# A group softmax bound by DMA: the first store waits until the fourth load has landed on every engine

## The chip, the cores and the metric

One NeuronCore of a Trainium2 chip. The metric is the device time of one execution in microseconds (us), the median of several. A profile gives one execution in detail; its span is some 2 us shorter than the time of the same execution.

## The reference

```python
B, N, D, G = 4, 4096, 4352, 8            # x is float32, 285 MB
x_g = x.reshape(B, N, G, D // G)         # groups of 544
exp = np.exp(x_g - x_g.max(axis=-1, keepdims=True))
out = (exp / exp.sum(axis=-1, keepdims=True)).reshape(B, N, D)
```

16,384 rows of 4,352 numbers are read once and written once, 570 MB in all.

## The kernel before

A tile is 128 partitions of two rows each, 4,352 KB. There are 64 tiles in five buffers. SyncE issues all transfers into one queue: four loads first, then for each tile t the store of t and the load of t + 4. I call them load 0 to load 63 and store 0 to store 63. In the queue the order is load 0, 1, 2, 3, store 0, load 4, store 1, load 5, and so on; from store 0 to store 60 every transfer changes direction against the one before it. I call such a change a turn.

```python
def take(engine, sem, n=1):
    engine.sem_inc(sem, -n).wait_op(sem, n, "sem-ge")
...
def load(t, source):
    nc.sync.dma_start(out=bufs[t % NT][:, :], in_=source).then_inc(landed[t % NT], 16)

def store(t, target):
    take(nc.sync, scaled, R)
    nc.sync.dma_start(out=target, in_=bufs[t % NT][:, :]).then_inc(stored[t % NT], 16)

def step(t, source, target):
    store(t, target)
    take(nc.sync, stored[(t - 1) % NT], 16)
    load(t + AHEAD, source)

for t in range(AHEAD):                    # AHEAD = 4, NT = 5
    load(t, xt[t])
nc.sync.sem_inc(stored[NT - 1], 16)
with nc.sync.Fori(0, ring_turns) as u:    # 12 ring turns of five steps
    for t in range(NT):
        step(t, turn_in[u, t], turn_out[u, t])
...
```

VectorE takes the maximum of each group and later multiplies by the reciprocal of the sum; ScalarE takes the exponential and the sum. Row by row this costs VectorE 9.6 us.

Of the kernel before, what the change touches and what calls it, by code (L numbers as in the profile page):

```python
# [1 line left out]

# [4 lines left out]


@with_exitstack
def kernel(  # L10
    ctx: ExitStack,
    tc: tile.TileContext,
    x: bass.AP,
    out: bass.AP,
):
    nc = tc.nc
    G = 8
    P = 128
    R = 2
    NT = 5  # L20
    S = R * NT
    AHEAD = NT - 1
    xf = x.flatten_outer_dims()
    of = out.flatten_outer_dims()
    N, D = xf.shape
    Dg = D // G
    nt = N // (P * R)
    nr = nt * R
    turns = (nr - 1) // S
    ring_turns = (nt - AHEAD) // NT  # L30
    steps = ring_turns * NT
    f32 = mybir.dt.float32
    X = mybir.AxisListType.X
    Exp = mybir.ActivationFunctionType.Exp
    xt = xf.rearrange("(t p r) d -> t p (r d)", p=P, r=R)
    ot = of.rearrange("(t p r) d -> t p (r d)", p=P, r=R)
    turn_in = xf[AHEAD * P * R:(AHEAD + steps) * P * R, :].rearrange(
        "(u b p r) d -> u b p (r d)", b=NT, p=P, r=R)
    turn_out = of[:steps * P * R, :].rearrange("(u b p r) d -> u b p (r d)", b=NT, p=P, r=R)

    landed = [tc.alloc_semaphore(f"landed{b}") for b in range(NT)]
    stored = [tc.alloc_semaphore(f"stored{b}") for b in range(NT)]

    max_done = tc.alloc_semaphore("max_done")
    exp_done = tc.alloc_semaphore("exp_done")
    rec_done = tc.alloc_semaphore("rec_done")
    scaled = tc.alloc_semaphore("scaled")

    ctx.enter_context(tc.tile_critical(no_gpsimd_drain=True))  # L49
    bufs = [ctx.enter_context(nc.sbuf_tensor(f"xt{b}", [P, R * D], f32)) for b in range(NT)]  # L50
    mx = ctx.enter_context(nc.sbuf_tensor("mx", [P, S, G], f32))
    sm = ctx.enter_context(nc.sbuf_tensor("sm", [P, S, G], f32))
    rs = ctx.enter_context(nc.sbuf_tensor("rs", [P, S, G], f32))

    def take(engine, sem, n=1):
        engine.sem_inc(sem, -n).wait_op(sem, n, "sem-ge")

    def row(s):
        b, r = divmod(s, R)
        return bufs[b][:, r * D:(r + 1) * D].rearrange("p (g d) -> p g d", g=G)  # L60

    def vector_max(s):
        i = nc.vector.reduce_max(out=mx[:, s, :], in_=row(s), axis=X, negate=True)  # L63
        if s % R == 0:
            i.wait_op(landed[s // R], 16, "sem-ge")
        i.then_inc(max_done, 1)

    def vector_scale(s):
        nc.vector.reciprocal(out=rs[:, s, :], in_=sm[:, s, :]).wait_op(  # L69
            exp_done, s + 1, "sem-ge").then_inc(rec_done, 1)  # L70
        xr = row(s)
        nc.vector.tensor_tensor(  # L72
            out=xr,
            in0=xr,
            in1=rs[:, s, :].unsqueeze(2).to_broadcast([P, G, Dg]),
            op=mybir.AluOpType.mult,
        ).wait_op(rec_done, s + 1, "sem-ge").then_inc(scaled, 1)

    def scalar_exp(s):
        xr = row(s)  # L80
        for g in range(G):
            i = nc.scalar.activation(  # L82
                out=xr[:, g, :],
                in_=xr[:, g, :],
                func=Exp,
                bias=mx[:, s, g:g + 1],
                scale=1.0,
                accum_out=sm[:, s, g:g + 1],
            )
            if g == 0:  # L90
                i.wait_op(max_done, s + 1, "sem-ge")
        i.then_inc(exp_done, 1)
# [14 lines that stand above are left out]
    for t in range(AHEAD):  # L107
        load(t, xt[t])
    nc.sync.sem_inc(stored[NT - 1], 16)
    with nc.sync.Fori(0, ring_turns) as u:  # L110
        for t in range(NT):
            step(t, turn_in[u, t], turn_out[u, t])
    for t in range(steps, nt):
        if t + AHEAD < nt:
            step(t, xt[t + AHEAD], ot[t])
        else:
            store(t, ot[t])
    for t in range(nt - NT, nt):
        nc.sync.wait_ge(stored[t % NT], 16)

    nc.scalar.preload_act_table(Exp)  # L121
    with nc.scalar.Fori(0, turns):
        for s in range(S):
            scalar_exp(s)
        nc.scalar.sem_inc(max_done, -S)
    for n in range(turns * S, nr):
        scalar_exp(n % S)


    vector_max(0)  # L130
    with nc.vector.Fori(0, turns):
        for s in range(S):
            if s == S - 1:
                for b in range(NT):
                    nc.vector.sem_inc(landed[b], -16)
            vector_max((s + 1) % S)
            vector_scale(s)
        nc.vector.sem_inc(exp_done, -S)
        nc.vector.sem_inc(rec_done, -S)
    for n in range(turns * S, nr):  # L140
        if n + 1 < nr:
            vector_max((n + 1) % S)
        vector_scale(n % S)


# [1 line left out]
_INS = ['x']  # L147
_OUTS = [((4, 4096, 4352), 'float32')]


# [23 lines left out]
```

## Time and profile before

| | before |
|---|---|
| time, median | 1330.15 us (1329.7 to 1330.15, 3 runs) |
| DMA queue, share of 16 engines | 99.7% |
| VectorE / ScalarE busy | 91% / 58% |
| one transfer, on the engine that is ahead | 10.28 us |

The prediction below shows the lines of the profile. Every transfer is spread over 16 DMA engines, and each of them adds one to the transfer's semaphore when its part has landed. The trace has the time of each increment. I call the first of the sixteen the leading engine's landing, the last one the straggler's, and the difference the spread. The trace also has each packet of 34,816 bytes with its duration, 1,024 for each engine, median 1.288 us. What a packet takes beyond that I call its excess; summed over a stretch of time and divided by 16 it is the time lost by an average engine. Packets don't carry an engine's number, so I can't say which engine is the straggler. A busy engine can be followed all the same, since each of its packets starts within a few ns of the end of the one before.

### The profile page before, as it was taken

How to read it: one execution, taken by the hardware profiler on the slowest of the kernel's cores; microseconds unless marked ns; L12 is line 12 of the kernel's file. 1: busy time of each engine (PE TensorE's matmuls, PEld its weight loads, DVE VectorE, ACT ScalarE, POOL GpSimd, SP SyncE). 2: the span in 40 equal slices, each digit the busy share in tenths (PEclk: the TensorE clock that was granted, in tenths of full speed). 3: DMA queues.
4: the chain of work that ended last, by engine and by line, in shares of the span. 5: the costliest groups of instructions: out<-in, count | busy, mean ns of one | idle time of the engine just before them, and what ended most of it. 6: DMA issues, size and time to landing. Idle time of an engine off the chain costs nothing. (4 is left out here: it accounts for less than half of the span.)

```text
span 1326.8 us, 3155 instructions
## 1 busy us (share of the span) xinstructions
DVE 1207.7 (91%) x384; ACT 764.4 (58%) x2049; POOL 0.2 (0%) x4
## 2 busy tenths in 40 slices
DVE  5999999999898898998988989889899898998984
ACT  3666565655565555655655556555565555655652
POOL 0000000000000000000000000000000000000000
DMA  9999999999999999999999999999999999999998
GB/s 403 419 431 433 429 430 430 436 433 429 431 433 436 433 431 430 435 435 436 431 431 433 436 433 433 430 432 436 435 433 429 433 436 436 431 430 433 435 435 358
DMA packets 18435, 570.46 MB, mean 430 GB/s; under 512 B 2048, under 2 KB 2048, under 8 KB 2048
## 3 DMA queue, kind: packets, MB, share of 16 engines
q1 hardware_dynamic: 18432, 570.43, 99.7%
q14 instruction: 3, 0.02, 0.0%
HBM read 285.21 MB, written 285.21 MB: 430 GB/s over the span
## 5 line engine op out<-in xcount | busy, mean ns | idle before, releaser
L82 ACT ACTIVATE xt<-xt,mx 128x544 f32<-128x544 f32 x1024 | 751.3, 734 | 539.2 <-DVE mx L63 539.2
L63 DVE TENSOR_REDUCE mx<-xt 128x8 f32<-128x4352 f32 x128 | 599.1, 4681 | 94.8 <-DMA xt<-in_x_dram 94.8
L72 DVE TENSOR_TENSOR xt<-xt,rs 128x4352 f32<-128x4352 f32 x128 | 600.6, 4692 | 4.4
L82 ACT ACTIVATION_READ_ACCUMULATOR xt<-xt,mx 128x1 f32 x1024 | 191.0, 187 | 0.0
L69 DVE RECIPROCAL rs<-sm 128x8 f32<-128x8 f32 x128 | 24.6, 193 | 2.6 <-ACT xt L82 2.6
L121 ACT ACT_TABLE_LOAD x1 | 1.3, 1283 | 0.9 <-SPq L49 0.9
L158 POOL MEMSET const-bfloat16-1.0<- 128x1 bf16 x1 | 0.1, 101 | 0.0
L158 POOL MEMSET const-uint8-127<- 128x1 uint8 x1 | 0.1, 101 | 0.0
L158 POOL MEMSET const-float32-0.0<- 128x1 f32 x1 | 0.1, 98 | 0.2 <-issue 0.2
L158 POOL MEMSET const-float32-1.0<- 128x1 f32 x1 | 0.1, 98 | 0.0
## 6 DMA issues: line engine op xcount, KB each, us to landing
xt<-in_x_dram SPq DMA_DIRECT2D x64, 4352.0 KB, 30.6
out_dram<-xt SPq DMA_DIRECT2D x64, 4352.0 KB, 40.3
```

The costliest lines, as they stand in the source:

```text
L63: i = nc.vector.reduce_max(out=mx[:, s, :], in_=row(s), axis=X, negate=True)
L69: nc.vector.reciprocal(out=rs[:, s, :], in_=sm[:, s, :]).wait_op(exp_done, s + 1, "sem-ge").then_inc(rec_done, 1)
L72: nc.vector.tensor_tensor(out=xr, in0=xr, in1=rs[:, s, :].unsqueeze(2).to_broadcast([P, G, Dg]), op=mybir.AluOpType.mult,).wait_op(rec_don ...
L82: i = nc.scalar.activation(out=xr[:, g, :], in_=xr[:, g, :], func=Exp, bias=mx[:, s, g:g + 1], scale=1.0, accum_out=sm[:, s, g:g + 1],)
L121: nc.scalar.preload_act_table(Exp)
L158: nc = _bacc.Bacc("TRN2", target_bir_lowering=False, num_devices=1)
```

## The change

The intent: the first store starts on all DMA engines together, since it is issued only when the last of the four first loads has landed on all of them.

```diff
     for t in range(AHEAD):
         load(t, xt[t])
     nc.sync.sem_inc(stored[NT - 1], 16)
+
+    nc.sync.wait_ge(landed[AHEAD - 1], 16)
     with nc.sync.Fori(0, ring_turns) as u:
```

## The prediction

> **What bounds the kernel now.** I read the page first (busy shares, DMA slices, queues), then SyncE's part of the timeline, the chain that ended last, the windows of the last 30 us, and last the sixteen completion increments that the trace holds for each transfer. The page:
>
> ```profile
> span 1326.8 us, 3155 instructions
> DVE 1207.7 (91%) x384; ACT 764.4 (58%) x2049; POOL 0.2 (0%) x4
> ...
> GB/s 403 419 431 433 429 430 430 436 433 429 431 433 436 433 431 430 435 435 436 431 431 433 436 433 433 430 432 436 435 433 429 433 436 436 431 430 433 435 435 358
> ...
> q1 hardware_dynamic: 18432, 570.43, 99.7%
> ...
> xt<-in_x_dram SPq DMA_DIRECT2D x64, 4352.0 KB, 30.6
> out_dram<-xt SPq DMA_DIRECT2D x64, 4352.0 KB, 40.3
> ```
>
> The one queue that carries all loads and stores occupies the 16 DMA engines for 99.7% of the span. VectorE is second at 91%. There are 64 loads and 64 stores of equal size, and a store lands 40.3 us after its issue because it stands behind earlier work in the queue. The kernel is bound by DMA. VectorE could become the bound only if DMA got 9% faster.
>
> How little is left: the trace holds 16,384 packets of 34,816 bytes, 1,024 for each engine, median 1.288 us. Eight of them are an engine's part of one transfer, and on the engine that is ahead one transfer follows the other at 10.28 us. 34,816 B / 1.286 us = 27.07 GB/s for one engine, 433 GB/s for sixteen. Only the first two slices and the last one of the GB/s row are clearly below that. SyncE's timeline shows what happens in the first:
>
> ```profile
> 0.96 1.99 SPq L96 DMA_DIRECT2D xt<-in_x_dram  x4
> 39.24 0.37 SPq L100 DMA_DIRECT2D out_dram<-xt  x1
> 39.86 0.35 SPq L96 DMA_DIRECT2D xt<-in_x_dram  x1
> 58.06 0.35 SPq L100 DMA_DIRECT2D out_dram<-xt  x1
> 58.67 0.35 SPq L96 DMA_DIRECT2D xt<-in_x_dram  x1
> ```
>
> Four loads (load 0 to 3) are issued at once; store 0 follows at 39.24, when tile 0 is scaled, and load 4 right behind it. Load 3 lands only at 45.08 to 46.00 (first to last engine). So store 0 is queued some 6 us before it can start, and each engine goes on to it by itself.
>
> The sixteen increments give the spread between the first and the last engine: 0.55, 0.54, 0.53 us for loads 0 to 2, 0.93 for load 3, 0.68 for store 0, 1.29 for load 4, then rising to 3.3 (150 us), 4.2 (210 us), 5.0 (318 us), and it stays at 5.0 until the end. One straggler causes the last 1.5 us or so of it: of the sixteen, the last but one is at 3.3 to 3.7. The end shows what it costs:
>
> ```profile
> 1310.00:1315.00 5.00, 0.00 (x0) 0.00 (x0) 0.00 (x0) 1.00 1.02 439
> 1315.00:1320.00 5.00, 0.00 (x0) 0.00 (x0) 0.00 (x0) 1.00 1.02 439
> 1320.00:1325.00 5.00, 0.00 (x0) 0.00 (x0) 0.00 (x0) 1.00 0.26 111
> ```
>
> Columns are the stretch, its length, VectorE, ScalarE and GpSimd work, clock, DMA share and GB/s. The last store lands on the first engine at 1321.09 and on the last at 1325.48; DMA share falls to 0.26 while the straggler finishes. The chain of waits ends like this:
>
> ```profile
> 1253.72 30.64 DMA xt<-in_x_dram
> ...
> 1284.39 4.68 DVE mx L63
> ...
> 1298.54 5.97 ACT xt L82 x16
> ...
> 1304.78 4.69 DVE xt L72
> ```
>
> The last load lands on the last engine at 1284.37, 25.1 us of compute follow, and the last store is issued at about 1309.56. The leading engines end the store before it near 1309.8 (landed 1310.16), so they starve for about 0.6 us; the straggler (landed 1315.20) does not. The straggler alone sets the end.
>
> **What the Trainium skill says.** Page "DMA: Bandwidth & Descriptors", section "Why a DMA increments its semaphore by 16 and not by 1": up to 16 engines finish independently and each posts one increment after its data. The trace agrees: 16 increments for each of the 128 transfers, up to 5.04 us apart. The same page, "Anatomy of one DMA": DMA engines do not wait on semaphores; a wait is on the issuing sequencer before dispatch. So the new wait can only delay the issue, and shows up as empty queues. Same page, "Where 436 GB/s comes from": a ceiling of 435.2 GB/s; the trace's steady 433 agrees, so nothing is to be had from rate. Same page, "Latency and other measured facts": about 600 ns to the first byte of a transfer issued from SyncE; the trace has 1.02 us for the first load (issue 0.96, first packet 1.98) and 0.8 us for the last store (1309.56 to 1310.38), and I use those.
>
> **The change part by part.** One wait is added; in the built program it sits on the branch into the loop, so no instruction is added, and nothing moves on the other engines.
>
> 1. The wait. Store 0 is ready at 39.24 and now goes after load 3 has landed on all engines. In its place are: (a) Without company in the queue, load 3 should take 10.28 us after load 2 (33.97 to 34.50), so it lands at 44.3 to 44.8. (b) From there to the first packets of store 0: the last store is the same case, with VectorE's end at 1309.47 and first packets at 1310.38 to 1310.47, 0.9 us; I add 0.2 for the branch into the loop. First packets at 45.9. (c) Store 0 then needs 10.28 + 0.35 us (last packet to increment, from 1325.13 to 1325.48): lands at about 56.5, within some 0.2 us on all engines. Before: 55.61 to 56.29. The leading engine loses 0.9 us, the straggler 0.2 us.
>
> 2. What pays for it. The last two packets of load 3 are long in the trace, 1.3 to 2.2 us against 1.288 (starts 41.2 to 43.5, about 2 us after store 0 and load 4 were issued). This cost the leading engine 11.11 - 10.28 = 0.8 us and the straggler 46.00 - 34.50 - 10.28 = 1.2 us. I take it that these vanish. So the hole of about 2 us (43.9 to 45.9 on a leading engine) is more than half paid by them.
>
> 3. The alignment. After 56.3 the straggler loses 5.04 - 0.68 = 4.4 us more against the leader. Its last increments show where: +0.4 at load 4, +0.3, +0.6, +0.5, +0.7 at the next loads, then +0.8 near 214 and +0.6 near 318, never at a store. The packets agree: long ones come in groups at 64, 85, 105, 126, 147 us, each the last packets of a load before the engine turns to a store, and the later an engine arrives, the longer (at 64.0 us +0.06, at 64.9 us +0.49). Nothing of this needs the start of store 0 to be staggered: each turn from load to store makes its own delay, and groups stop when the engines have moved apart. If so, beginning at 0.2 instead of 0.68 us only means that the spread grows again to about the same size.
>
> Sum: the leader goes from 55.61 to 56.5, all turns after that are the same, and the final spread decides. At 5.0 us again the end comes 0.9 us later; at 4.2, 0.1 us later; at 3.3 us, 0.8 us earlier. Compute does not enter: store 1 is issued at 58.06 when its tile is scaled, as before, and tile 4 is needed by VectorE only near 86 us, against a landing at 67.
>
> **The rivals.** First, the intent holds: engines that begin together stay together, the spread stays under 1 us to the end. Then the end is 0.2 - 4.4 = about -4 us: 1326. For it: loads 0 to 2 do keep a spread of 0.54. Against it: these are load after load; the spread grows at every turn from load to store, and there are 64 of them. Second, being aligned makes the turn at load 4 as dear as the one at load 3 was (all sixteen in step, 0.8 to 1.2 us each), and the spread ends at 6 to 7: +1.5 to +2.5 us, 1332. For it: the dear turn was the one with the smallest spread. Third, the hole delays the supply: load 5 waits for store 0. Store 0 now lands at 56.5, and load 5 was issued at 58.67 behind store 1 anyway, so this is hidden: 0. Fourth, VectorE as bound: it gets its first tile at 13.90 as before and waits only later; 0.
>
> **Range and chances.** I weigh: same final spread (0 to +1 us) 0.4, smaller spread (-2 to 0) 0.25, larger (+1 to +2.5) 0.2, drift gone (-4) 0.15. Centre about -0.1 us from 1330.15: 1330.0 us. The range runs from 1326.4 to 1332.0. Two per cent is 26.6 us; the first 60 us hold no such sum, and no state but one is known for one core. Faster 0.01, within 0.98, slower 0.01.
>
> **What would show it.** In the changed trace: store 0 issued near 45 instead of 39.24, with load 4 0.6 us after it; no long packets at the end of load 3; a hole of about 2 us in DMA near 44 to 46; store 0 landing at about 56.5 with a spread under 0.3 us. Then long packets at the turns near 65, 86 and 106, and a spread that grows to 3 to 6 us by 320 us. The prediction is wrong if the spread stays small (about 1326) or grows past 7, or if the hole is longer than 3 us.

## The result, and the profile after

| | before | changed |
|---|---|---|
| time, median | 1329.93 us (1329.07 to 1330.15, 4 runs) | 1332.28 us (1331.81 to 1332.63, 4 runs) |
| ratio to before | | 1.0019, 95% interval 1.0001 to 1.0036: the same at 2% |
| span of the profiled run | 1326.8 us | 1330.4 us |

A ratio is the mean time of one kernel's fast runs over that of the other's of the same rounds, so it is not quite the ratio of the medians. The loss is 2.35 us in the medians. The predicted range ended at 1332.0; the measured time lies 0.28 us above it.

The page of the changed kernel, the lines that answer to those of before:

```profile
span 1330.4 us, 3155 instructions
...
GB/s 402 385 422 427 432 431 433 428 430 430 432 431 434 435 435 432 430 430 434 433 435 434 434 433 430 431 433 433 435 435 434 433 428 432 434 433 435 433 434 364
...
q1 hardware_dynamic: 18432, 570.43, 99.6%
```

The second slice of the GB/s row, about 33 to 67 us, falls from 419 to 385, the third from 431 to 422; the fourth is 6 lower and the fifth 3 higher, and from there on the rows are alike. 34 GB/s less in 33 us is 1.1 MB, which 433 GB/s moves in 2.6 us; the 9 of the third slice are another 0.7. So nearly all of the loss is made before 100 us. SyncE's timeline (start, duration, what):

```profile
0.96 1.92 SPq L96 DMA_DIRECT2D xt<-in_x_dram  x4
45.56 0.37 SPq L100 DMA_DIRECT2D out_dram<-xt  x1
46.19 0.35 SPq L96 DMA_DIRECT2D xt<-in_x_dram  x1
57.98 0.35 SPq L100 DMA_DIRECT2D out_dram<-xt  x1
58.59 0.35 SPq L96 DMA_DIRECT2D xt<-in_x_dram  x1
```

and SyncE's waits (who waited for what, total us, times, longest):

```profile
SPq L112 <- DMA xt<-in_x_dram: 42.2, 1, 42.2
```

The new wait ends at 45.56 and store 0 is issued there, 6.3 us later than before; store 1 and load 5 keep their times. The next two fences are windows of the two kernels, before and then after. Their columns are the stretch, its length, work of VectorE, ScalarE and GpSimd, clock, DMA share and GB/s. A packet counts whole in the window in which it starts, so a share can be over 1. Undisturbed packets give a share of 1.00 for each 433 GB/s, or 1.29 beside 557 and 0.65 beside 279; a share well above that means long packets.

```profile
40.00:42.00 2.00, 2.00 (x1) 0.13 (x2) 0.00 (x0) 1.00 1.44 540
42.00:44.00 2.00, 1.97 (x3) 0.39 (x1) 0.00 (x0) 1.00 0.99 279
44.00:46.00 2.00, 2.00 (x1) 2.00 (x7) 0.00 (x0) 1.00 0.65 279
46.00:48.00 2.00, 2.00 (x1) 2.00 (x6) 0.00 (x0) 1.00 1.21 522
...
54.00:56.00 2.00, 2.00 (x1) 2.00 (x7) 0.00 (x0) 1.00 1.01 435
...
64.00:66.00 2.00, 2.00 (x1) 2.00 (x6) 0.00 (x0) 1.00 1.08 435
66.00:68.00 2.00, 2.00 (x2) 2.00 (x7) 0.00 (x0) 1.00 1.01 435
```

```profile
40.00:42.00 2.00, 2.00 (x1) 0.06 (x1) 0.00 (x0) 1.00 1.21 522
42.00:44.00 2.00, 1.97 (x3) 0.47 (x1) 0.00 (x0) 1.00 0.69 296
44.00:46.00 2.00, 2.00 (x1) 2.00 (x7) 0.00 (x0) 1.00 0.00 0
46.00:48.00 2.00, 2.00 (x1) 2.00 (x7) 0.00 (x0) 1.00 1.32 557
...
54.00:56.00 2.00, 2.00 (x1) 2.00 (x7) 0.00 (x0) 1.00 1.67 557
...
64.00:66.00 2.00, 2.00 (x1) 2.00 (x6) 0.00 (x0) 1.00 1.44 557
66.00:68.00 2.00, 2.00 (x2) 2.00 (x7) 0.00 (x0) 1.00 0.90 279
```

Before, the long packets lie at 40 to 44 (1.44 for 540 GB/s, then 0.99 for 279): these are the last two packets of load 3, the last but one from 41.2 on. After, they are gone from there, the window 44 to 46 has no packet starting at all, and long packets stand at 54 to 56 (the last packet of store 0; on most engines the first of load 4 behind it is long too) and 64 to 68 (the last two of load 4). Worked out from the traces, the excess of an average engine in us (all traces of each kernel, the later ones from the experiments):

```
                                   before (3 traces)     changed (3 traces)
turn load 3 to store 0 (36-48 us)  1.09  1.09  1.01      0.08  0.08  0.08
turn store 0 to load 4 (54-60 us)  0.00  0.07  0.00      0.99  0.93  0.91
turn load 4 to store 1 (64-72 us)  0.15  0.28  0.08      0.83  0.82  0.99
next turns (72-112 us)             0.24  0.45  0.69      0.31  0.13  0.52
after that, to 330 us              0.77  1.03  1.29      1.56  1.21  1.08
```

One dear turn (one with much excess) has become two, and there is a hole besides, a time in which the queue is empty. The end, by landings (us; the means are over four traces of before, the fourth being the control wait_third below, and three of the changed kernel):

```
                                   before                  mean     changed               mean
store 0, leading engine            55.61 55.86 55.72 55.70  55.72   57.73 57.75 57.36     57.61
load 4, leading engine             65.70 66.05 65.68 65.69  65.78   68.96 68.97 68.74     68.89
store 62, leading engine (1300 +)  10.16 10.74 10.64 10.03  10.39   13.84 13.49 13.58     13.64
spread at store 62                  5.04  5.17  6.62  6.04   5.72    4.95  5.96  4.45      5.12
store 63, straggler (1300 +)       25.48 26.18 27.51 26.35  26.38   29.05 29.72 28.29     29.02
```

The leading engine is 1.9 us late at store 0, 3.1 us at load 4, and 3.25 us at the end: all of it is there by load 4. The final spread is the same within its own scatter. The end is 2.6 us later in these traces, which agrees with the 2.35 us of the timed runs. The first trace of before, from which I predicted, was one of the quickest of its kernel.

### The profile page after: what moved, and what is told of

Read it like the earlier page. It is cut to its first block, busy times and chain, and to the rows that moved or that the text cites. A ratio compares the mean times of both kernels' runs of the same rounds, so it can differ in the third digit from the quotient of the medians.

```text
span 1330.4 us, 3155 instructions
## 1 busy us (share of the span) xinstructions
DVE 1207.9 (91%) x384; ACT 764.5 (57%) x2049; POOL 0.2 (0%) x4
## 3 DMA queue, kind: packets, MB, share of 16 engines
q1 hardware_dynamic: 18432, 570.43, 99.6%
```

## The experiments

Theory A, at first: the hole in the queue costs time, and behind it the turns are dear because all engines make them together. Rivals: the wait's code costs (B), the hole alone costs (C), one engine is slow by itself (D), a restart makes any transfer slow (E), each change of direction costs always (F).

### The changed kernel again, and the same wait where it does not bind

```diff
-    nc.sync.wait_ge(landed[AHEAD - 1], 16)
+    nc.sync.wait_ge(landed[AHEAD - 2], 16)    # wait_third; after_again has no edit
```

> The changed kernel once more, beside the others. Both theories: 2.0 to 3.5 us slower than the kernel before (ratio 1.0015 to 1.0026); store 0 lands on the first engine near 57.7 us, and the spread at the end is again between 4 and 6 us. If the loss was noise between runs, the ratio is within 1.0005 of 1.

> The same wait at the same place, but on the third load, which lands at 34.5 us, before store 0 is ready at 39.2. Theory A (the hole in the queue and, after it, turns that all engines take together cost the time): the wait does not bind, so the kernel is as before, ratio 1.000 within 0.0007, store 0 issued near 39.2 us and landing from 55.6 us. Rival B (the wait on the branch into the loop itself, as code, costs): 1 to 3 us slower, as the changed kernel.

Measured: after_again 1332.7 us against 1330.4 for before, ratio 1.0016 (1.0002 to 1.0029). wait_third 1329.57, ratio 0.9998 (0.9985 to 1.0012), store 0 issued at 39.27 and landing from 55.70, excess at the turn from load 3 1.08 us. The loss repeats, and it needs the wait to bind; the code of the wait costs nothing that these runs show. B falls.

### The wait in every ring turn

```diff
-    nc.sync.wait_ge(landed[AHEAD - 1], 16)
     with nc.sync.Fori(0, ring_turns) as u:
+        nc.sync.wait_ge(landed[AHEAD - 1], 16)
```

> The wait moved into the loop, so that the queue runs empty before each of the 12 ring turns (10 transfers each) and all engines begin the next store together 12 times. Theory A: each costs the hole (1.6 us net as after the first) plus the aligned turns (2.0 us) plus the spread that has grown within 10 transfers (about 1 us, as at 110 us in the changed kernel), so 12 times 4 to 5 us less the 5 us of final spread that is kept small: 45 to 60 us slower, with long packets at the first turns of each ring turn. Rival C (the hole alone costs, turns cost the same however the engines stand): 12 times 1.6 to 2.4 us, 15 to 30 us slower.

Measured: 1387.93 us, 57.5 us slower, ratio 1.0432 (1.0416 to 1.0448). Its windows around the second hole:

```profile
150.00:152.00 2.00, 2.00 (x1) 2.00 (x7) 0.00 (x0) 1.00 0.41 174
152.00:154.00 2.00, 2.00 (x2) 1.27 (x4) 0.00 (x0) 1.00 0.00 0
154.00:156.00 2.00, 2.00 (x1) 0.00 (x0) 0.00 (x0) 1.00 0.91 383
...
162.00:164.00 2.00, 2.00 (x1) 0.70 (x2) 0.00 (x0) 1.00 1.65 557
```

No packet starts from 152 to 154 (on the last engine the hole is 153.3 to 154.7), and 10 us later the same long packets stand at the end of the store (1.65 for 557 GB/s), as at 54 to 56 after the first hole. Between landings of the store behind one hole and behind the next there are 108.4, 108.8 and 107.9 us, against 102.8 for ten undisturbed transfers. In the trace the two turns behind each of the twelve holes have 0.8 to 1.0 and 0.9 to 1.3 us of excess, the four behind them at most 0.4 each. So hole and dear turns come together each time. The time lies where A put it and far over C.

### The hole without turns

```diff
-        nc.sync.dma_start(out=target, in_=bufs[t % NT][:, :]).then_inc(stored[t % NT], 16)
+        nc.sync.dma_start(out=bufs[t % NT][:, :], in_=target).then_inc(stored[t % NT], 16)
```

(with target a part of x; every store becomes a load into the same tile, the result is wrong. loads_only has no wait, loads_only_wait has that of the change.)

> The kernel before with every store replaced by a load of the same size into the same tile (a wrong result on purpose; out is never written), so the queue holds the same 128 transfers at the same waits and no engine ever turns from load to store. Theory A (the straggler is made at the turns): no long packets after the start, the spread of the sixteen increments stays near 0.5 us from the first transfer to the last, and the end comes 4 to 6 us earlier: 1324 to 1326. Rival D (one engine is slower by itself, or drifts whatever it moves): the spread grows to 4 to 6 us all the same and the time is within 1.5 us of the kernel before.

> The same without stores, with the wait of the change: the hole by itself, without turns. Theory A: the last engine loses from the landing of load 3 to the first packets of the next transfer, about 1.3 us, plus the 0.35 us from last packet to landing, and nothing later: 1.5 to 2.7 us slower than loads_only. Rival E (the restart itself makes the next transfers slow, whatever they are): 3.5 us or more slower than loads_only, with long packets at the end of the transfer after the hole.

Measured: loads_only 1328.4 us, 0.9987 of before; loads_only_wait 1331.56 us. The spread of loads_only goes from 0.42 to 0.99 us at load 3 and stays at 1.0 to 1.1 to beyond 1100 us (1.8 at the end). So most of the straggler's distance is made where loads and stores alternate, and D falls. The time was a miss: 1.1 us faster in place of 4 to 6. Its cause is in the trace: a load here follows a load at 10.315 us, where the alternating queue has 10.283; 124 times 0.032 is 4.0 us.

The hole by itself costs 3.16 us in the medians. The windows of loads_only_wait:

```profile
44.00:46.00 2.00, 2.00 (x1) 2.00 (x7) 0.00 (x0) 1.00 0.00 0
46.00:48.00 2.00, 2.00 (x1) 2.00 (x6) 0.00 (x0) 1.00 0.96 279
```

Here the packets at the restart itself are long, by 0.5 to 1.1 us from 46.6 on (0.96 for 279 GB/s), as those of load 0 are at 2 us. Store 0 in the changed kernel starts at the same time without that: its first packets are long by 0.02 us. That is why the hole alone came out over my 1.5 to 2.7 us, though under the 3.5 of E. There is no excess at the end of the transfer behind the hole, and none at the next: both dear turns are missing where nothing turns. So they belong to turns and not to any transfer after a restart, and E falls as it was put. One variant of it was not tested apart: in loads_only_wait the first load after the empty queue pays 0.6 us per engine, and in the changed kernel the first load behind the hole is load 4. Part of the first dear turn may be that same cost.

### Engines put apart ahead of the first turn

Now theory A's second half: are these turns dear because the engines come together? The turn from load 5 to store 2 in the changed kernel speaks against it: 0.14 us, though store 1 before it had landed with a spread of only 0.51. A first attempt put seven small loads behind the wait:

```diff
     nc.sync.wait_ge(landed[AHEAD - 1], 16)
+    p0 = 0
+    for k in range(14, 0, -2):
+        nc.sync.dma_start(out=bufs[NT - 1][p0:p0 + k, :D], in_=xf[:k, :]).then_inc(extra, 16)
+        p0 += k
     # step 0 follows, with a wait on extra ahead of load 4
```

> The wait stays, and behind it seven small loads of 14, 12, ... 2 partitions (17 KB each, thrown away) go ahead of store 0, so that the engines begin store 0 up to 4.5 us apart in steps of 0.64 us. The hole is longer by the seven issues, about 2.6 us, and the leading engine starts store 0 near 49 us in place of 46.4. Theory A: with the engines apart, the turns cost next to nothing: from the leading engine's first packet of store 0 to its landing of the last store but one there are 1265.1 us without any delay, and this kernel shows 1265 to 1266, where the changed kernel shows 1267.4; the spread starts at 4.5 and stays under 5.5; time within 1.5 us of the changed kernel although its hole is 2.6 us longer. Rival C (turns cost the same however the engines stand): 1267.4 us there, spread growing by another 4 us to 8 to 9, and 5 to 7 us slower than the changed kernel.

Measured: 1340.13 us, 7.4 us slower than the changed kernel of the same rounds (1332.7), where I had said 1.5; the small loads landed only at 60.0 and load 4, which waits for them, was issued at 60.08, when the leading engines had run dry. A miss of design. It shows one thing: store 0 landed with a spread of 10.8 us, and from load 4 to beyond 1000 us the spread stayed at 8.2 to 8.3 (8.9 at the end) with the leading engine at 10.28 us for each transfer. Two more attempts cut load 0 into pieces, without any wait:

```diff
-        load(0, xt[0])
+    # uneven_first_load: 112 partitions in one load; the last 16, row by row, in loads of 14, 10, 6, 2
+    # uneven_first_load_wide: 96 partitions in one; the last 32, both rows, in loads of 14, 10, 6, 2
```

> The kernel before, no wait; the last 16 partitions of load 0 are cut into four small loads of 14, 10, 6 and 2 partitions, one row each, [...]the engines leave load 0 about 2.6 us apart in steps of 0.64, and the busiest has 1.3 us more than an even share. Result correct. Theory A: the turn at load 3 costs less than the 0.8 to 1.2 us of before, and since the engines are apart already the straggler gains less than the 4.4 us of before; spread at the end 3 to 5 us; 0 to 3 us faster than before. Rival D: the 2.6 us come on top of the usual 5 to 6, spread 7 to 8 at the end, 1 us slower or more.

> The same with 32 partitions cut into loads of 14, 10, 6 and 2 partitions of both rows: engines leave load 0 about 5.2 us apart in steps of 1.3, the busiest has 2.6 us above an even share. Result correct. Theory A: almost no long packets at any turn, spread stays at 5 to 6 us from load 0 on, the leading engine's landings follow at 10.28 us throughout; since the busiest engine is only 2.6 us above an even share, 1 to 3 us faster than before. Rival D: spread 9 to 11 at the end, 2 us slower or more.

Measured: 1340.54 us (1.0079) and 1353.55 us (1.0169), both far off. The cut loads crawl, the large piece too. In the wide one packets of the load of 96 partitions took 2.3 to 2.7 us between 5 and 15 us in place of 1.29, those behind it up to 5.6, and the last of the small loads landed at 38.3 us; from there on packets were normal again. Its windows:

```profile
10.00:20.00 10.00, 0.00 (x0) 0.00 (x0) 0.00 (x0) 1.00 1.04 185
20.00:30.00 10.00, 0.00 (x0) 0.00 (x0) 0.00 (x0) 1.00 1.08 111
```

The engines count as busy all the time (1.04 and 1.08), and move 185 and 111 GB/s in place of 433. The first store was issued at 53.6 and 63.7 us. Why they crawl was not tested. These two say nothing on turns.

Copies inside HBM avoid the partitions. They go from x to rows of out that the right result overwrites later (16 rows each in the even ones):

```diff
+    q0 = (nt - 1) * P * R
+    for k in (14, 12, 10, 8, 6, 4, 2):          # even: seven times 16; four: 14, 10, 6, 2
+        nc.sync.dma_start(out=of[q0:q0 + 2 * k:2, :], in_=xf[q0:q0 + 2 * k:2, :]).then_inc(extra, 16)
+        q0 += 2 * k
     # copies_*: ahead of load 3, no wait.  wait_then_copies_*: behind the wait of the change
     # copies_uneven_half: the same seven, half a row each
```

> The kernel before, no wait, with the seven uneven copies between load 2 and load 3, so that the engines come to their first turn, load 3 to store 0, some 4 us apart. Alignment: long packets at that turn under 0.3 us for each engine (1.09 in the kernel before), and the spread grows little from there. First turn: 1 us for each engine all the same. Time: the busiest engine has 7 small copies more, 4.5 us or more, so -1 to +5 us against the kernel before.

> The same with seven copies of 16 rows on all engines between load 2 and load 3: all engines still come to the turn from load 3 to store 0 together, some 5 us later. Alignment: about 1 us of long packets for each engine at that turn. If the copies themselves take the place of the first turn: under 0.4 us there. Time 4 to 10 us slower than the kernel before.

> Behind the wait, seven small copies from x to the last rows of out (written over at the end by the right result) of 14, 12, ... 2 rows go ahead of store 0; they use as many engines as they have rows, so the engines begin store 0 apart, by 4 us or more. Alignment: the turns from store 0 to load 4 and from load 4 to store 1 show under 0.3 us of long packets for each engine (1.0 and 0.8 to 1.0 in the changed kernel). First turns after the hole: about 1 us and 0.9 us for each engine as before, spread out in time. Time: 2 to 8 us slower than the kernel before, which decides nothing.

> The same with seven copies of 16 rows each, on all 16 engines, so that the engines begin store 0 together again, about 5 us later. Alignment: about 1 us and 0.9 us for each engine at the same two turns. First turns after the hole: the copies are now the first work after the hole, which read and write HBM, so the turns that follow may be cheap, under 0.4 us each. Time 5 to 10 us slower than the kernel before.

Measured, with the excess of an average engine at the turns as in the table above:

```
                          time us  ratio    spread at    turn 3 to S0  S0 to L4  L4 to S1   later, to 330
                                            store 0
copies_uneven             1331.11  1.0006      5.05          1.14        0.00      0.00        0.05
copies_even               1334.31  1.0031      1.67          0.74        0.00      0.05        0.93
wait_then_copies_uneven   1341.19  1.0083      1.13           -          0.96      1.03        0.96
wait_then_copies_even     1338.92  1.0066      1.92           -          0.03      0.43        0.78
```

copies_uneven decides it. Its engines come to the first turn up to 5.0 us apart, and the first turn costs 1.14 us for each all the same. Followed engine by engine, all sixteen lose 0.8 to 1.4 us: eleven on the last two packets of load 3, the five that come last one or two packets earlier. These packets start between 41.6 and 47.1 us, against 41.2 to 43.5 in before. So that turn is not dear because the engines make it together; that half of theory A falls. That the late engines pay a little ahead of their own turn hints that they are not wholly independent; this stays open. What holds in its place: the first turn after the start, and the first two after the hole, cost about 1 us each. wait_then_copies_uneven has them again behind the hole, 0.96 and 1.03; its copies failed to put the engines far apart (they are issued at about 0.76 us each, as slowly as they run), 1.13 us in place of the 4 or more expected, and its time is a miss too, 11.0 us over before in place of 2 to 8. Most of its engines ran dry a second time, from the end of their copies at 47.7 to 51.1 to the first packets of store 0 at 51.7. wait_then_copies_even has nearly lost them, 0.03 and 0.43: there seven copies on all 16 engines, which read and write HBM, were the first work after the hole. That is as the second reading expected, but it is one run. copies_even, with such copies between load 2 and load 3 and no hole, came out between its two outcomes (1 us, or under 0.4): 0.74 us at the first turn, and 0.46 us more on the first packets of load 3 behind the copies. Why work after an empty queue makes its first turns dear I have not settled.

copies_uneven also shows what distance does. With engines 5 us apart no later turn costs anything, 0.05 us against 1.0 to 2.0 in before between 72 and 330 us, and the spread stays at 5.1 us to beyond 700, where before needed 320 us to drift there. wait_then_stagger, 8.2 us apart, agrees: 0.06 us between 112 and 330. So up to 330 us the later, small delays come with a small spread, and they make the straggler. It is not the whole account: from some 750 us on the spread of copies_uneven grows again, to 6.7 us at the end, and no run here tells why.

### More traces, and stores in a queue of their own

before_again_a, before_again_b and after_third are copies without an edit. stores_on_own_queue issues the stores from ScalarE, behind the exponentials of the row that comes after the tile is scaled.

> The kernel before, for a second trace. Unprofiled it took 1329.5 to 1330.4 us in the median where its first trace (1328.73) was among the quickest. If the final spread is what moves one run against another, this trace has a span near 1328 and a final spread near 6 us in place of 5.0, with the leading engine landing the last store but one again near 1310 us.

> The same, a third trace: leading engine at 1310 within 0.3 us, final spread anywhere between 5 and 7 us, span following it one for one.

> The changed kernel, a third trace: leading engine lands the last store but one at 1313.7 within 0.3 us (1313.84 and 1313.49 so far), 3.5 us after that of the kernel before; final spread between 4.5 and 6.5 us (4.95 and 5.96 so far).

> The kernel before with its stores issued from ScalarE, so that loads and stores stand in two queues and each engine takes packets of both in turn; result correct. Theory A (a turn from load to store costs when many engines make it together): there are no common turns any more, so the spread stays under 3 us and the time is 1 to 5 us below the kernel before. Rival F (every change of direction costs an engine something, together or not): there are now up to 1,024 of them for each engine in place of 124, so it is slower by 20 us or more. A third outcome, within 1 us, says that mixing has a price of its own near the 5 us of spread.

The traces are in the tables above. Three expectations missed by little: the leading engine of before came at 1310.74 and 1310.64 against 1310 within 0.3, the spread of before_again_a was 5.17 in place of some 6, and that of after_third 4.45, just under its 4.5 to 6.5. stores_on_own_queue took 1330.01 us, ratio 0.9996 (0.9979 to 1.0013), with the work halved between two queues:

```profile
q1 hardware_dynamic: 9216, 285.22, 49.9%
q10 hardware_dynamic: 9216, 285.22, 49.7%
```

The third outcome of the text: its spread is 2.6 us at 370 us in place of 5 to 6, but one engine drifts on to 4.95 by the end, and the last stores land together at 1327.0 to 1327.2. Followed engine by engine, 64% of the packets between 60 and 120 us and 87% of those between 900 and 960 us come from the other queue than the one before them, so there are some hundreds of changes of direction for each engine in place of 121, and they cost no 20 us. F falls, and nothing is won.

### Can the start be set better?

> As copies_uneven with copies of half a row (8.7 KB): the engines come to load 3's end about 2.6 us apart in steps of 0.33, and the busiest has 2.3 us more to do. The first turn costs about 1 us for each engine again. If a spread of 2.6 us is enough to keep the later turns free, the spread stays under 4 us to the end and the time is 1.5 to 3 us below the kernel before (about 1328); if not, it grows to 5 to 6.5 us as before and the time is within 1 us of it.

> Four copies of whole rows on 14, 10, 6 and 2 engines: also about 2.6 us apart, in steps of 0.65 with up to four engines on one step. The same two outcomes; if steps matter more than the whole distance, the spread stays smaller here than with half rows (under 4 us against 5 or more).

Measured: 1330.88 us (1.0011, 0.9997 to 1.0024) and 1330.23 us (1.0005, 0.9992 to 1.0019). The first turn costs 0.94 and 1.1 us again. The spread is 3.2 to 3.3 us at store 0, but 4.0 and 4.85 at 610 us and 5.4 and 5.9 at the end. Half the distance slows the drift and doesn't stop it. copies_uneven_half is 1.6 us over before, where the text allowed 1. No version here beats the kernel before.

## Why the prediction was wrong

- The bound: right. The queue stays at 99.6%, the computing engines' rows are unchanged, and the straggler's last store sets the end.
- Step 1, the wait: nearly right. Store 0 was issued at 45.56 in place of 39.24, no instruction was added, and first packets came at 46.43 against 45.9. Load 3 lands on the straggler at 45.17 against 44.8, the issue came 0.39 us after it, and the first packet 0.87 us after that. This is 0.5 us of the miss.
- Step 2, the long packets at the end of load 3 vanish: right, from 1.09 to 0.08 us.
- Step 1(c), "Store 0 then needs 10.28 + 0.35 us ... lands at about 56.5, within some 0.2 us on all engines": this step failed. It landed at 57.73 to 58.28. On the leading engine 57.73 - 46.43 - 10.28 - 0.35 leaves 0.67 us for a long last packet that the sum did not have. Step 3 had read the trace of before as delays "never at a store"; here the first dear turn is at the end of a store.
- The sum, "The leader goes from 55.61 to 56.5, all turns after that are the same": this failed with it. The turn from load 4 to store 1 has 0.8 to 1.0 us of excess against 0.1 to 0.3, and the leading engine's distance grows from 1.9 us at store 0 to 3.1 us at load 4 in the means. I had booked the dear turn of load 3 as saved. In truth the hole pays it back twice, at the first two turns behind it.
- The second rival, with a chance of 0.2, was right on the size of the turn ("as dear as the one at load 3 was") and of the loss (+1.5 to +2.5; measured 2.35), and wrong on the reason and the final spread: the turn costs all engines alike, and the spread does not end at 6 to 7. So its size was partly luck. copies_uneven shows that being together is not the reason.
- The weighing: the middles of its four cases (+0.5, -1, +1.75, -4) with their chances give -0.3 us and not "about -0.1". This changes nothing above.
- Step 3, the alignment: right. Starting together did not keep the engines together; the spread grew to 4.5 to 6.0 us against 5.0 to 6.6. The first rival, that the drift is gone, did not come.
- The third and fourth rivals: no effect, as predicted. Load 5 was issued at 58.59.

So the hole was about right and the final spread was right, and the missing term is two turns of about 1 us. 0.9 + 0.5 + 0.67 gives 2.07 of the 2.12 us at store 0 in the first traces, and the long packets of load 4, its first and its last two, add about 1.2. What stays open is why the first turns after an empty queue are dear. First work that reads and writes HBM on all engines took most of it away in one run, which may come from the copies themselves or from the load behind them no longer being the first; no run tells more.

## What to carry to other kernels

In this queue, 99.7% busy, a wait on the issuing engine bought only a hole, and the hole cost more than its own length: it was 1.7 us long on the last engine and 2.6 us on the first, and the first two turns from one direction to the other behind it took 0.8 to 1.0 us each on all engines. Against that stood one dear turn saved. Engines that started together (a spread of 0.55 to 0.65 us at store 0) did not stay together where loads and stores alternate, so aligning them was not a gain that lasted. To find a loss of 2 us in 1330, compare landings of the same transfer between several traces of each kernel: the profiled run alone was 1.4 us quicker than its kernel's median.

## What the Trainium skill lacked or had wrong

- "DMA: Bandwidth & Descriptors" (Specifications) gives about 27 GiB/s for one engine; the traces show 27.07 GB/s (34,816 bytes in 1.286 us), which is 25.2 GiB/s. Sixteen of them are 433 GB/s, which agrees with the page's 435.2.
- The same page (Latency and other measured facts) gives about 600 ns to the first byte for SyncE; here 0.8 to 1.0 us from the start of the issue to the first packet.
- No page has the drift: with loads and stores in turn the sixteen engines of one core end 4.5 to 6.6 us apart, with loads alone 1.8 us.
- No page has the cost of turns after an empty queue: 1.0 to 1.1 us for each engine at the first turn after the start, 0.9 to 1.0 and 0.8 to 1.0 at the first two after the hole, at most 0.3 at the two right behind them (0.4 in wait_each_turn).
- "HBM Reference" (Specifications) gives about 425 GB/s for one core alone; the queue of loads and stores in turn held 433 in its steady part and loads alone 432 (4.46 MB in 10.315 us).
